# Prompt attention scores of a hybrid decoder: one 128-query matmul becomes four 32-query matmuls in four column groups

## The chip, the cores and the metric

The kernel runs on one core of one Trainium2 chip. The metric is the device time of one execution in microseconds (us), median of several runs. A profile is one execution, with its own time.

## What is computed

One inference step of a two-layer decoder for 512 prompt tokens and 8 samples of 4 tokens (544 tokens in all, model width 1024), in float32. In each layer the input projection `x @ w_in` feeds four mixers (a gated convolution A, a gated delta rule B, a gated linear attention C, a differential attention D with relative bias); their outputs are joined, projected by `w_o` and normalised, and a channel mixer follows (a dense SwiGLU in layer 0, a mixture of eight experts in layer 1). The change touches only the prompt part of mixer D:

```python
def _diff_attn_core(q, k, v, q_pos, k_pos, lam, rel_bias):
    s = jnp.einsum('bqhmd,bkhmd->bmhqk', q, k).astype(jnp.float32) * (HEAD_DIM_DQK ** -0.5)
    bias = jnp.transpose(rel_bias[_t5_bucket(q_pos, k_pos)], (2, 0, 1)).astype(jnp.float32)
    s = jnp.where(k_pos[None, :] <= q_pos[:, None], s + bias, -jnp.inf)
    p = jax.nn.softmax(s, axis=-1)
    w = p[:, 0] - lam * p[:, 1]
    return jnp.einsum('bhqk,bkhv->bqhv', w.astype(v.dtype), v)
```

There are four heads, each with two score maps (m = 0 and 1) of depth 32, and queries come in blocks of 128.

## The kernel before

One program does both layers in turn. `mixers` (L480) traces, in this order: `d_in` (projections d_q, d_k, d_v), `b_in` (L744: projections of B, convolutions, norms), `b_chunks` (L836: the delta rule), `d_attn` (L592, called at L1322: attention of the prompt and of the samples), `c_in` (L1116: projections of C), then `b_sample`, `mix_a`, `mix_c`. Projections go through `dense` (L383): for each tile of weights 48 matmuls into a tile `st`, with weights and activations each split into a high and a low part (`wh`, `wl`, `xh`, `xl`). All matmuls are issued by the helper `mm` (L291 and L292), so the profile shows them at L292 and tells them apart by their tiles.

`d_attn` alternates steps of `d_sample` (L608) with heads of the prompt: after step n of `d_sample` it traces heads until their number reaches (n+1)*16/20. A step of `d_sample` loads pages of the cache (tile `pg`) and makes scores with queries `qs` and outputs with probabilities `kv`; its matmuls come in fours, for four samples b, each into partitions 32b to 32b+31 of one PSUM tile. Another group of four of this kind, for the new tokens of the samples, multiplies `etn` with `vt` (L686). There, as in the change, 32 rows and 32 columns of the array are used by each matmul, all four have the same moving operand, and the output is 256 wide.

`d_head` (L708) is one query block (qb = 0 to 3) of one head: 16 calls in a layer, 32 in all. For each m it takes a PSUM tile from the pool `dx` (three buffers) and makes the scores: the stationary operand is 32 x 128 (q, tile `y`), the moving one 32 x nk (k, tile `arr`), with nk = 128, 256, 384 or 512 by the query block. So there are 64 score matmuls, 16 of each width. Behind them come the bias (VectorE, L295), the maximum (L726), the exponential (ScalarE, L728), the two weights, four or fewer transposes on TensorE (L736), a copy (L737) and the matmuls with `vt`.

A float32 matmul stands in the trace as two MATMUL records and two weight loads; a matmul of `st` (type fp32r) as one of each.

The order of instructions in each engine's queue is not that of the text. It is written when the program is built: `tile.TileContext(nc, schedule_with_timeline_sim=True)` (L2155) has a planner run the program on a clock of its own, and whenever an engine is free there, the planner gives it, of the instructions whose operands and buffers are there by that clock, the one that was traced first. On the chip each engine works its queue off in that order.

Of the kernel before, what the change touches and what calls it, by code (L numbers as in the profile page):

```python
# [267 lines left out]
def _body(ctx, tc, I, O):  # L268
# [22 lines left out]
    def mm(out, lhsT, rhs, start=True, stop=True):  # L291
        return PE.matmul(out, lhsT, rhs, start=start, stop=stop)  # L292

    def tt(e, out, a, b, op):
        return e.tensor_tensor(out, a, b, op=op)  # L295
# [184 lines left out]
    def mixers(l, y32, hook):  # L480
# [8 lines left out]
        def mx():  # L489
            return xps.tile([128, 512], F32, name="mx")  # L490

        def dx():
            return dps.tile([128, 512], F32, name="dx")
# [214 lines left out]
        def d_head(q, k, vt, qb, tl, h2):  # L708
            od = y32[:, 6:8]
            nk = 128 * (qb + 1)  # L710
            q0 = 128 * qb
            b0 = max(0, q0 - 128)
            h = 2 * tl + h2
            hp = slice(64 * h2, 64 * h2 + 64)

            def go():
                zz = dq.tile([128, 8], F32, name="zp", bufs=2)
                e, pss = [], []
                for m in range(2):
                    p0 = h2 * 64 + m * 32  # L720
                    ps = dx()
                    mm(ps[:, 0:nk], q[p0:p0 + 32, tl, q0:q0 + 128], k[p0:p0 + 32, tl, 0:nk])
                    pss.append(ps)
                for m, ps in enumerate(pss):
                    tt(V, ps[:, b0:nk], ps[:, b0:nk], bt[:, h, 256 - (nk - b0):256], OP.add)
                    V.reduce_max(zz[:, m:m + 1], ps[:, 0:nk], axis=AX.X, negate=True)  # L726
                    em = dq.tile([128, 512], F32, name="kv", bufs=KVB)
                    S.activation(em[:, 0:nk], ps[:, 0:nk], AF.Exp, bias=zz[:, m:m + 1], accum_out=zz[:, 2 + m:3 + m])  # L728
                    e.append(em)
                V.reciprocal(zz[:, 4:6], zz[:, 2:4])  # L730
                tt(V, zz[:, 5:6], zz[:, 5:6], neglam[:, l:l + 1], OP.mult)
                S.activation(e[1][:, 0:nk], e[1][:, 0:nk], AF.Copy, scale=zz[:, 5:6])
                V.scalar_tensor_tensor(e[0][:, 0:nk], e[0][:, 0:nk], zz[:, 4:5], e[1][:, 0:nk], op0=OP.mult, op1=OP.add)
                po, pw = pss
                for kb in range(qb + 1):
                    PE.transpose(pw[:, kb * 128:(kb + 1) * 128], e[0][:, kb * 128:(kb + 1) * 128], ident)  # L736
                S.activation(e[1][:, 0:nk], pw[:, 0:nk], AF.Copy)  # L737
                for kb in range(qb + 1):
                    mm(po[hp, 0:128], vt[:, kb, h * 64:h * 64 + 64], e[1][:, kb * 128:(kb + 1) * 128], start=kb == 0, stop=kb == qb)
                V.tensor_copy(od[hp, tl, q0:q0 + 128], po[hp, 0:128])  # L740

            return go
# [566 lines left out]
        if l:  # L1309
# [4 lines left out]
            ps = mx()  # L1314
# [853 lines left out]
```

## Time and profile before

| | us |
|---|---|
| median of 3 runs | 2140.98 |
| lowest and highest | 2140.56 to 2145.11 |
| profiled execution | 2135.03 |
| its span, first to last instruction | 2133.4 |
| mean granted TensorE clock in it | 0.958 |

The page of the profile has engine busy times, the span in 40 slices, DMA queues and the costliest groups. The stretches in which the heads of the prompt are worked on are 40 to 360 us (layer 0) and 985 to 1310 us (layer 1). In a timeline the start of a MATMUL group and the start of the group behind it tell what the group took of the engine's time: the records' own durations run on past that, since matmuls are pipelined.

### The profile page before, as it was taken

Reading aid. Unit: us, or ns where it says so; the run is one execution under the profiler, and the core shown is the slowest. Engines: PE = TensorE matmul, PEld = TensorE weight load, DVE = VectorE, ACT = ScalarE, POOL = GpSimd, SP = SyncE. Lnnn points to the kernel's source line nnn. Section 1 sums busy time; section 2 is a strip of 40 time slices with the busy share of each in tenths; the row PEclk is TensorE's granted clock in tenths of the full one; section 3 lists DMA queues with packets and bytes.
Section 4 is the critical chain, followed back from the end, with each engine's and each line's share of the span. In section 5 each row is a group of like instructions: output and inputs, shape, how many; then the busy total and the mean of one; then the engine's idle time right before and its main releaser. Section 6 shows DMA issues by size and latency. Waiting matters only on the chain. (4 is left out here: it accounts for less than half of the span.)

```text
span 2133.4 us, 46787 instructions
## 1 busy us (share of the span) xinstructions
PE 2001.4 (94%) x17620; PEld 1800.9 (84%) x17620; DVE 1298.2 (61%) x2588; ACT 946.4 (44%) x1826; POOL 375.2 (18%) x544
## 2 busy tenths in 40 slices
PE   8999989998999999989999999995999999999895
PEld 7877647987999999978687658985999999999894
DVE  4566555567333333653566566566887878767875
ACT  3444234544322223432544234534666666665441
POOL 1220032202000000031120032101220303403532
PEclk9999998989999999999999989996999999999998
DMA  6456551323222322545554543134778878787851
GB/s 238 147 155 178 148 165 42 94 88 92 90 87 75 102 85 81 150 135 170 162 150 135 170 122 99 43 109 160 230 257 307 298 224 300 228 284 258 289 182 64
DMA packets 183924, 340.93 MB, mean 160 GB/s; under 512 B 28035, under 2 KB 103912, under 8 KB 183688
## 3 DMA queue, kind: packets, MB, share of 16 engines
q1 hardware_dynamic: 160744, 287.67, 42.7%
q0 software_dynamic: 13968, 48.04, 7.2%
q10 hardware_dynamic: 8976, 2.13, 0.5%
q8 instruction: 141, 2.31, 0.4%
q14 instruction: 95, 0.78, 0.1%
HBM read 319.91 MB, written 17.85 MB: 158 GB/s over the span
## 5 line engine op out<-in xcount | busy, mean ns | idle before, releaser
L295 DVE TENSOR_TENSOR wl<-wraw,wh 128x1024 fp32r<-128x1024 f32 (+2 forms) x474 | 550.8, 1165 | 338.7 <-ACT wh L371 328.9
L371 ACT ACTIVATE wh<-wraw 128x1024 fp32r<-128x1024 f32 (+2 forms) x474 | 463.3, 980 | 493.9 <-PE st L292 267.5
L292 PE MATMUL st<-xh,wh 128*128 128x256 f32 (+1 forms) x1536 | 460.2, 300 | 20.6 <-ACT wh L371 7.6
L292 PE MATMUL st<-xl,wh 128*128 128x256 f32 (+1 forms) x1536 | 457.2, 298 | 4.0 <-DVE xl L295 4.0
L292 PE MATMUL st<-xh,wl 128*128 128x256 f32 (+1 forms) x1536 | 455.6, 297 | 4.0 <-DVE wl L295 3.8
L292 PEld LDWEIGHTS st<-xh,wh 128*128 128x128 f32 x1536 | 298.5, 195 | 37.5 <-ACT wh L371 7.7
L292 PEld LDWEIGHTS st<-xh,wl 128*128 128x128 f32 x1536 | 298.7, 195 | 14.7 <-issue 8.4
L292 PEld LDWEIGHTS st<-xl,wh 128*128 128x128 f32 x1536 | 299.1, 195 | 13.3 <-issue 7.8
L292 PE MATMUL st<-xg,wh 128*128 128x416 f32 (+4 forms) x880 | 237.9, 351 | 1.3 <-DVE m_u L1746 0.7
L292 PE MATMUL st<-xg,wl 128*128 128x208 f32 (+4 forms) x880 | 211.8, 241 | 0.0
L292 PEld LDWEIGHTS st<-xg,wl 128*128 128x128 f32 x880 | 168.0, 191 | 0.0
L292 PEld LDWEIGHTS st<-xg,wh 128*128 128x128 f32 x880 | 165.3, 188 | 2.7 <-issue 0.8
L292 PE MATMUL st<-hg,wh 128*128 128x416 f32 (+4 forms) x440 | 122.3, 355 | 0.1
L292 PE MATMUL st<-hg,wl 128*128 128x208 f32 (+4 forms) x440 | 107.9, 247 | 1.7 <-DVE wl L295 1.7
L1481 POOL TENSOR_SCALAR r<-r,par 128x256 f32<-128x256 f32 (+1 forms) x32 | 30.5, 966 | 446.4 <-ACT xh L1480 446.4
L292 PE MATMUL ff<-hh,wl 128*128 128x256 f32 (+1 forms) x352 | 102.4, 294 | 4.6 <-DVE wl L295 4.6
L292 PE MATMUL st<-wh,xg 128*128 128x256 f32 x528 | 105.5, 293 | 0.0
L292 PE MATMUL ff<-hh,wh 128*128 128x256 f32 (+1 forms) x352 | 102.5, 292 | 1.6 <-ACT wh L371 1.6
L292 PE MATMUL ff<-xh,wh 128*128 128x256 f32 (+1 forms) x352 | 102.5, 291 | 0.5 <-ACT wh L371 0.5
L292 PE MATMUL ff<-xl,wh 128*128 128x256 f32 (+1 forms) x352 | 102.4, 291 | 0.0
L292 PE MATMUL ff<-xh,wl 128*128 128x256 f32 (+1 forms) x352 | 102.2, 291 | 0.0
L292 PE MATMUL ff<-hl,wh 128*128 128x256 f32 (+1 forms) x352 | 101.8, 290 | 0.0
(581 smaller groups left out, 3956.1 us busy)
## 6 DMA issues: line engine op xcount, KB each, us to landing
pg<-in_kc_dram SPq DMA_DIRECT2D x256, 128.0 KB
pg<-in_vc_dram SPq DMA_DIRECT2D x256, 128.0 KB
wraw<-in_w_in_dram POOLq DMA_DIRECT2D x56, 512.0 KB, 4.3
wraw<-in_m_g_dram SPq DMA_DIRECT2D x54, 512.0 KB
wraw<-in_m_u_dram SPq DMA_DIRECT2D x54, 512.0 KB
wraw<-in_m_g_dram SPq DMA_DIRECT2D x65, 256.0 KB
wraw<-in_m_u_dram SPq DMA_DIRECT2D x65, 256.0 KB
wraw<-in_w_o_dram SPq DMA_DIRECT2D x32, 512.0 KB
```

The source lines that it names most:

```text
L292: return PE.matmul(out, lhsT, rhs, start=start, stop=stop)
L295: return e.tensor_tensor(out, a, b, op=op)
L371: S.activation(h, r, AF.Copy)
L1481: G.tensor_scalar(ri[:, u], ri[:, u], gcol[:, u:u + 1], bcol[:, u:u + 1], op0=OP.mult, op1=OP.add)
```

## The change

The one matmul of 128 queries becomes four of 32 queries. Each writes 32 partitions of the same PSUM tile and streams the same keys.

```diff
                 for m in range(2):
                     p0 = h2 * 64 + m * 32
                     ps = dx()
-                    mm(ps[:, 0:nk], q[p0:p0 + 32, tl, q0:q0 + 128], k[p0:p0 + 32, tl, 0:nk])
+                    for c in range(0, 128, 32):
+                        mm(ps[c:c + 32, 0:nk], q[p0:p0 + 32, tl, q0 + c:q0 + c + 32], k[p0:p0 + 32, tl, 0:nk])
                     pss.append(ps)
```

## Rows read from the trace of the kernel before

**Rows 1.** The page, part 1: busy us, share of span, instructions.

```profile
PE 2001.4 (94%) x17620; PEld 1800.9 (84%) x17620; DVE 1298.2 (61%) x2588; ACT 946.4 (44%) x1826; POOL 375.2 (18%) x544
```

**Rows 2.** Windows of both attention stretches: stretch, length, busy of each engine, clock, DMA.

```profile
40.00:360.00 320.00, 300.08 (x2949) 225.84 (x2948) 182.84 (x486) 126.07 (x293) 52.85 (x120) 0.95 0.52 150
985.00:1310.00 325.00, 308.76 (x3041) 235.28 (x3040) 190.07 (x512) 131.32 (x313) 57.27 (x130) 0.95 0.48 140
```

**Rows 3.** Waits of PE, 40 to 360 us: the longest in total; total, times, longest.

```profile
PE dx L292 <- DMA pg<-in_kc_dram: 7.4, 5, 2.9
```

**Rows 4.** Groups of instructions by form: the score matmuls.

```profile
L292 PE MATMUL dx<-arr,y 32*128 32x512 f32 x32 | 17.2, 673 | 0.0
...
L292 PE MATMUL dx<-arr,y 32*128 32x384 f32 x32 | 14.5, 533 | 0.0
...
L292 PE MATMUL dx<-arr,y 32*128 32x256 f32 x32 | 11.1, 426 | 0.0
...
L292 PE MATMUL dx<-arr,y 32*128 32x128 f32 x32 | 7.6, 332 | 0.0
```

**Rows 5.** Timelines of PE: start us, us; one score matmul of each width, its follower.

```profile
107.13 0.48 PE L292 MATMUL dx<-arr,y 32*128 32x128 f32 x2
107.54 0.40 PE L292 MATMUL st<-xh,wh 128*128 128x288 f32 x1
...
146.52 0.69 PE L292 MATMUL dx<-arr,y 32*128 32x256 f32 x2
147.14 0.39 PE L292 MATMUL st<-xh,wl 128*128 128x256 f32 x1
...
251.80 0.91 PE L292 MATMUL dx<-arr,y 32*128 32x384 f32 x2
252.64 0.73 PE L292 MATMUL mx<-lt,inv 64*64 64x64 f32 x9
...
288.75 1.12 PE L292 MATMUL dx<-arr,y 32*128 32x512 f32 x2
289.80 0.83 PE L292 MATMUL dx<-pg,qs 128*32 128x256 f32 x9
```

**Rows 6.** Timeline of PE: a group of four in one piece.

```profile
350.99 0.63 PE L292 MATMUL dx<-vt,etn 32*32 32x256 f32 x8
351.56 0.25 PE L292 MATMUL mx<-kq 64*32 64x32 f32 x4
```

**Rows 7.** Timelines of PE: the same group of four, other samples; then layer 1.

```profile
206.74 0.61 PE L292 MATMUL dx<-vt,etn 32*32 32x256 f32 x2
207.28 0.65 PE L292 MATMUL dx<-kv,vt 128*64 128x128 f32 x4
207.86 0.63 PE L292 MATMUL dx<-vt,etn 32*32 32x256 f32 x6
...
1147.18 0.61 PE L292 MATMUL dx<-vt,etn 32*32 32x256 f32 x2
```

**Rows 8.** Timelines of PE: first and last score matmuls followed by earlier text.

```profile
42.91 0.49 PE L292 MATMUL dx<-arr,y 32*128 32x128 f32 x4
43.33 0.40 PE L292 MATMUL st<-xh,wh 128*128 128x288 f32 x1
...
1244.34 1.13 PE L292 MATMUL dx<-arr,y 32*128 32x512 f32 x4
1245.40 0.92 PE L292 MATMUL dx<-pg,qs 128*32 128x256 f32 x10
```

**Rows 9.** Tile dx: weight loads, duration min/median/max in ns.

```profile
L292 PEld LDWEIGHTS dx<-arr,y x128: 181/184/332, 42.9 to 1288.6; 32*128 32x128 f32 x128
...
L292 PEld LDWEIGHTS dx<-vt,etn x32: 101/103/105, 206.7 to 1284.4; 32*32 32x32 f32 x32
```

**Rows 10.** Tile dx: who waited for it (us, times).

```profile
  DVE dx L295: 26.4, 32
```

## Prediction

> **What bounds the kernel now.** I read the page's busy times first. TensorE is busy for 94% of the span, VectorE for 61%, ScalarE for 44% [rows 1], so the first question is what the change does to TensorE's queue. An average hides stages, so I then asked for windows of the two stretches that hold all heads of the prompt. There TensorE is busy for 300.1 of 320 us and 308.8 of 325 us, while VectorE has 182.8 and 190.1, and the DMA engines are about half busy [rows 2]. The list of TensorE's waits names no large one: the longest entry of layer 0 is 7.4 us, for pages of the cache [rows 3]. So in both stretches TensorE is the bound, with 36 us of idle time in 645 us (5.6%), and what is added to its queue arrives in the end time nearly whole.
>
> The score matmuls themselves are small: by the table of groups by form they add up to 17.2 + 14.5 + 11.1 + 7.6 = 50.4 us of busy time in both layers [rows 4], and that counts the pipelined tails. What one takes of the queue is read from the timeline, from its start to the start of what follows: 0.41 us at 128 keys, 0.62 at 256, 0.84 at 384, 1.05 at 512 [rows 5]. Each further 128 keys cost 0.21 us, so streaming takes 0.21, 0.43, 0.64 and 0.85 us, and 0.2 us are fixed.
>
> **What the change does, part by part.** It removes 64 matmuls and adds 256, so TensorE has 384 more MATMUL records and as many more weight loads. Nothing else is edited: VectorE's bias addition still waits for the whole tile, now for the last of four matmuls.
>
> *If the four stay together.* The nearest row is the group of four with `etn`: the same 32 rows and 32 columns for each matmul, one moving operand for all four, 256 wide. Its eight records take from 350.99 to 351.56, 0.57 us [rows 6]. Eight records in a line would take at least 4 x 0.43 = 1.7 us of streaming, so the four column groups do run at the same time. Against 0.62 us for one matmul of 128 queries of that width [rows 5] that saves 0.05 us. The weight loads show where it comes from: 184 ns for 128 columns, 103 ns for 32 [rows 9], a difference of 81 ns of which the staggered start of the four takes some back. It does not depend on the width, so 64 x 0.05 to 0.06 = 3.2 to 3.8 us; I take -3.5.
>
> The Trainium skill ("TensorEngine Tiling (Array Packing)", Performance Considerations, When to Use Tiling) names column tiling for a stationary operand of at most 64 columns; here it has 128, which fill the array already. By that rule the four gain nothing over the one, and the sum below would be 3.5 us higher. The row shows a small gain, from the load and not from packing.
>
> *If the planner parts the four.* Four instructions can be parted, one cannot. The planner gives a free TensorE the instruction that was traced first among those that are ready, and two of the four `etn` groups show what follows: one matmul at 206.74, then two matmuls `dx<-kv,vt` of an earlier-traced head, then the other three at 207.86; in layer 1 the same happens at 1147.18 [rows 7]. On the chip the second of four starts some ns behind the first, so the planner's clock must give the first a slot of its own that is long enough for the other work to become ready in it. I take it that this clock runs the four in a line. A piece that stands alone is dear: the single `etn` matmul holds the queue from 206.74 to 207.28, 0.54 us, hardly less than all four together, since it streams all the keys. With 0.21 us for each 128 keys, one more piece costs 0.33, 0.54, 0.75 or 0.97 us at 128, 256, 384 or 512 keys.
>
> How often? In the timeline I looked up what follows each of the 64 score matmuls. An instruction from earlier text means that it was ready, by the planner's clock, when the score matmul ended; after the change that is the end of the first quarter, and the planner will put it ahead of the other three. That is so for 29 of 64: 14 of 16 at 128 keys, 2 at 256, 5 at 384, 8 at 512. Mostly these are projections and norms of B, steps of `b_chunks`, and `d_sample` steps that were traced before the head; the first is the pair at 42.91, followed by `st`, the last the pair at 1244.34, followed by `dx<-pg,qs` [rows 8]. The other 35 are followed by later text (projections of C, mostly, as at 147.14 in [rows 5]) and can stay whole. One cut each: 14 x 0.33 + 2 x 0.54 + 5 x 0.75 + 8 x 0.97 = 17.2 us. If what is left is cut again with the same share (29/64 = 0.45), the factor is 1 + 0.45 + 0.21 = 1.66, and it is 28.5 us. With the saving of 3.5: +13.7 to +25.0. I take the middle, +19, and 1 us less for the share of idle time that may swallow it: +18.
>
> The outer bounds: no cut at all, -3.5; all 64 cut into four pieces, 3 x 16 x (0.33 + 0.54 + 0.75 + 0.97) = +124.
>
> *What is queued behind.* The bias addition on VectorE waits for the last piece; it waited 26.4 us for `dx` in 32 waits [rows 10], on an engine with 40% to spare, so that costs nothing by itself. It does hold one of the three `dx` buffers longer, and the next head or step of `d_sample` waits for that buffer on TensorE. The cover is other TensorE work; I cost it at nothing and leave the loss to the second rival.
>
> **The rivals.**
>
> *The four stay together* (ends on the other side). The price is -3.5 us: 2137.5. It decides by the length of the planner's slot for one quarter: if that is a few ns, nothing becomes ready in it. For it: two of the four `etn` groups are whole [rows 6]. Against it: the two cut ones. By the rule of the skill above it would be 2141.
>
> *The planner's clock misleads it* (slower than the forecast). If the planner runs the four in a line, it counts 3 x 16 x (0.21 + 0.43 + 0.64 + 0.85) = 102 us more on TensorE than the chip needs. The softmax behind a head then seems covered by TensorE work which on the chip is soon over, and TensorE waits at the transposes of L736 or at pages. TensorE's idle time of 36 us in both stretches [rows 2] would grow; with a quarter of the 102 us, +25 on top of the forecast: 2184. For it: that clock, if rows 7 are read rightly. Against it: there is other work between the steps of a head (in rows 5 projections follow at once).
>
> *The four run in a line on the chip.* +102 us: 2243. Rows 6 speak clearly against it, but there the moving operand lies in partitions 0 to 31 only.
>
> *Another order by chance.* A changed order moves all work behind it; TensorE's waits for pages and for weights could shrink by some us. That gives about 2132.
>
> **How the numbers follow.** The profiled execution took 2135.0 us, 6 us (0.3%) below the median of 2141.0 us; the sum is made on its span, and I add it to the median, as the rows' durations do not depend on that difference. Forecast, cut in part: 2141 + 18 = 2159, chance 0.52 (from +5 to +40, with a tenth of it within 0.2%). Together: 0.20, half of it within 0.2% and half beyond it, as -3.5 us is 0.16%. Misled planner: 0.18. In a line: 0.04. By chance lower: 0.06. A change of under 0.2% (4.3 us) can hardly be told from none here. Faster by more than that: 0.10 + 0.04 = 0.14; the same: 0.10 + 0.05 + 0.01 = 0.16; slower: 0.70. The range leaves out the serial case, the upper part of the misled planner and the lowest few: 2134 to 2200.
>
> **What would show it.** In the timeline of the changed kernel, score matmuls stand as `32*32 32x512 x8` in one piece, or as x2, x4 and x6 with other tiles between. On the timeline, a piece of eight at 512 keys should take about 1.0 us and a piece of two nearly as much. Counting pieces gives the added TensorE time directly: pieces beyond 64, times the prices above. The window rows should show more TensorE busy time in both stretches, of about the size of the loss; if the loss comes with more idle time instead, the second rival is right. The prediction is wrong if nearly all stand in one piece, or if eight records at 512 keys take about 3.5 us.

## The result, and the profile after

The changed kernel takes 2151.86 us (median of 20 executions, 2139.91 to 2169.41), the kernel before, run beside it, 2139.91 us (20 executions, 2128.76 to 2160.54). The ratio is 1.0075 with a 95% interval of 1.0057 to 1.0094: 16 us slower, 12 to 20 (the two medians by themselves lie 12 us apart). All ratios here leave out executions more than 1.5% above the fastest of their kernel, which is one, the 2174.73 us below. The forecast was 18 us slower. The time came out as forecast, but, as the runs below show, not for the reason that was given; the sum landed near the time by coincidence.

The page of the changed kernel's profile: part 1 (busy us, share of the span, instructions), and the line of part 2 with the granted clock in 40 slices; its span is 2155.5 us, against 2133.4 before. The last line is the clock in the kernel before:

```profile
PE 2023.4 (94%) x18004; PEld 1807.2 (84%) x18004; DVE 1300.1 (60%) x2588; ACT 946.2 (44%) x1826; POOL 375.9 (17%) x544
...
PEclk9999988999999999999998787997999999999997
...
PEclk9999998989999999999999989996999999999998
```

Against [rows 1] TensorE is 22.0 us longer busy, as much as the span grew (22.1 us); VectorE, ScalarE and GpSimd have the busy time they had, to 2 us. The prediction had named just this as its sign. But a busy TensorE may have more to do, or do the same at a lower clock, and the 8, 7, 8, 7 in the slices from 1132 to 1347 us, in layer 1's attention, where the kernel before has 9, 9, 8, 9 in the same slices, point to the clock. The windows of the two stretches (length, busy of each engine, PEclk, DMA share, GB/s), which answer to [rows 2]:

```profile
40.00:360.00 320.00, 301.18 (x3047) 219.31 (x3047) 180.72 (x477) 122.21 (x279) 50.52 (x118) 0.93 0.51 150
985.00:1310.00 325.00, 309.49 (x3067) 230.71 (x3066) 180.92 (x484) 121.61 (x282) 51.68 (x116) 0.89 0.46 139
```

In layer 1 the clock is 0.89 where it was 0.95, and VectorE gets 484 instructions done where it got 512 done: the stage is behind. (In fixed windows TensorE's busy time hardly moves; a slower stage just runs on past the window's end.)

The score matmuls by form (busy us, mean ns), which answer to [rows 4]:

```profile
L292 PE MATMUL dx<-arr,y 32*32 32x384 f32 x128 | 18.7, 580 | 0.0
L292 PE MATMUL dx<-arr,y 32*32 32x512 f32 x128 | 14.7, 657 | 0.0
L292 PE MATMUL dx<-arr,y 32*32 32x256 f32 x128 | 11.4, 386 | 0.0
L292 PE MATMUL dx<-arr,y 32*32 32x128 f32 x128 | 6.3, 280 | 0.0
```

And pieces of TensorE's timeline (start, us, tile, count), which answer to [rows 5] and [rows 8]; they come in order of time, with gaps:

```profile
42.51 0.43 PE L292 MATMUL dx<-arr,y 32*32 32x128 f32 x10
42.86 0.40 PE L292 MATMUL st<-xh,wh 128*128 128x288 f32 x1
...
73.99 0.41 PE L292 MATMUL dx<-arr,y 32*32 32x128 f32 x6
74.33 0.40 PE L292 MATMUL st<-xh,wh 128*128 128x288 f32 x1
...
86.80 0.42 PE L292 MATMUL dx<-arr,y 32*32 32x128 f32 x8
87.15 1.19 PE L292 MATMUL mx<-row,cst 128*128 128x256 f32 x4
...
171.10 0.63 PE L292 MATMUL dx<-arr,y 32*32 32x256 f32 x8
171.67 0.40 PE L292 MATMUL st<-xh,wl 128*128 128x288 f32 x1
...
228.26 0.84 PE L292 MATMUL dx<-arr,y 32*32 32x384 f32 x6
229.03 1.05 PE L292 MATMUL dx<-pg,qs 128*32 128x256 f32 x10
230.01 0.83 PE L292 MATMUL dx<-arr,y 32*32 32x384 f32 x2
230.77 0.39 PE L292 MATMUL st<-xh,wh 128*128 128x256 f32 x1
...
294.32 1.06 PE L292 MATMUL dx<-arr,y 32*32 32x512 f32 x8
295.31 0.44 PE L292 MATMUL mx<-gst,arr 64*128 64x64 f32 x4
```

Three readings. A whole group (x8) holds the queue for 0.35, 0.57 and 0.99 us at 128, 256 and 512 keys; the one matmul took 0.41, 0.62 and 1.05 [rows 5]. So 0.05 to 0.06 us are saved, as predicted. A group that is cut, as at 228.26, takes 0.77 + 0.76 us in two pieces where a whole one of 384 keys takes 0.78: the price of a lone piece, 0.75, is as predicted too. But cuts are few. In TensorE's queue, as the planner wrote it, 55 of the 64 groups stand whole, among them that at 86.80, though `mx<-row,cst`, text traced earlier, follows it. Cut are nine, each once: three at 128 keys, three at 256, three at 384, none at 512. (The x10 at 42.51 is a whole group and the first quarter of the next, whose other three follow at 73.99.) They cost at most 3 x (0.33 + 0.54 + 0.75) = 4.9 us. Three more look broken in the timeline, where records of small matmuls of other tiles start between those of one group; in the queue these are whole. Groups give back 64 x 0.06 = 3.8 us. So neither the cuts nor the new shape make 16 us.

Where they are lost, the clock shows. Windows of 1167 to 1208 us, first of the kernel before, then of the changed one (same columns as above):

```profile
1167.00:1208.00 41.00, 40.81 (x577) 30.50 (x576) 23.80 (x46) 12.72 (x27) 1.38 (x4) 0.96 0.51 154
...
1167.00:1208.00 41.00, 40.12 (x382) 26.74 (x383) 15.98 (x32) 8.18 (x18) 0.00 (x0) 0.50 0.29 85
```

TensorE is busy all through in both, yet in the changed kernel the granted clock is 0.50, the lower of its two levels (1.2 GHz), for the whole 41 us, and it has 382 MATMUL records in place of 577. The program alone does not fix this. The changed kernel was profiled once more (`changed_again` below), and there the same window reads:

```profile
1167.00:1208.00 41.00, 40.21 (x510) 28.61 (x512) 24.65 (x52) 14.30 (x31) 2.12 (x3) 0.97 0.49 143
```

So one stretch of one execution shows that the clock can cost this much, and not what costs it. What does differ between the two programs in every execution, beside the shape, is the order: the planner has written another one. Compared instruction by instruction, with a group of four counted as one, TensorE's queue differs from its 536th matmul on, in 3574 of 14586 places; VectorE's differs in 845 of 2588, ScalarE's in 379 of 1749.

### The profile page after: what moved, and what is told of

It reads as the page before. It is cut to its first block, busy times and chain, and to the rows that moved or that the text cites. A ratio compares the mean times of both kernels' runs of the same rounds, so it can differ in the third digit from the quotient of the medians.

```text
span 2155.5 us, 47593 instructions
## 1 busy us (share of the span) xinstructions
PE 2023.4 (94%) x18004; PEld 1807.2 (84%) x18004; DVE 1300.1 (60%) x2588; ACT 946.2 (44%) x1826; POOL 375.9 (17%) x544
## 5 line engine op out<-in xcount | busy, mean ns | idle before, releaser
L295 POOL TENSOR_TENSOR m_g<-m_g,m_u 128x208 f32<-128x208 f32 (+4 forms) x55 | 50.9, 926 | 303.4 <-DVE m_u L1747 270.4
```

## The experiments

Three causes could be told apart: (A) the order that the planner wrote for all other work, (B) the new shape of the matmuls itself, (C) the cuts. For that I wrote the queue order of every engine out, by edges that say only "after this one", so that shape and order can be combined at will. A group of four counts there as one unit, so none is cut. Each kernel is timed beside the kernel before on the same chip.

**The new shape in the order of before.** The edit is the change itself, and the order of the kernel before (`ORDER_OF` holds it for each engine):

```diff
+    edge = mybir.DependencyInfo(mybir.DependencyClass.NoSync, mybir.DependencyReason.DATA)
+    for e, s in ORDER_OF.items():
...
+        for a, b in zip(seq, seq[1:]):
+            tc.add_manual_dep(b, a.name, edge, reason="order")
```

> The scores are made by four matmuls of 32 queries as in the changed kernel, but every engine's queue keeps the order of the kernel before; each group of four stands in one piece where the one matmul stood. Theory A (the loss of 0.75% comes from the new order that the planner wrote, by way of a granted clock that stays at half speed longer): the order is the old one, so 2136 to 2141 us, ratio 0.998 to 1.000, half-speed time near the 183 us of before. Theory B (32 x 32 matmuls by themselves lower the granted clock or run slower in this place): about 2152, ratio 1.005 to 1.009, half-speed time well over 183 us in both attention stretches. Theory C (the loss is what cut groups cost): 2136 to 2141, as no group is cut.

Measured: 2137.2 us (2128.55 to 2144.63, 12 executions) against 2142.5 (35): ratio 0.9969, interval 0.9945 to 0.9992. The new shape alone makes the kernel faster, by 5 us (1.7 to 11.8 by the interval), which takes in the 3.5 us of the sum. B falls.

**The old shape in the order of the changed kernel.** Edges as above, now from the changed kernel's queues, around the one matmul of 128 queries. Beside the edges it differs from the changed kernel in this:

```diff
-                    for c in range(0, 128, 32):
-                        mm(ps[c:c + 32, 0:nk], q[p0:p0 + 32, tl, q0 + c:q0 + c + 32], k[p0:p0 + 32, tl, 0:nk])
+                    mm(ps[:, 0:nk], q[p0:p0 + 32, tl, q0:q0 + 128], k[p0:p0 + 32, tl, 0:nk])
```

> The scores are made by one matmul of 128 queries as before, but every engine's queue has the order of the changed kernel; where a group of four was cut there, the one matmul stands at the place of the first piece. Theory A (order): 2150 to 2158 us, ratio 1.005 to 1.009. Theory B (shape): about 2140, ratio 0.998 to 1.002. Theory C (cuts): about 2140, as there is nothing to cut.

Measured: 2158.77 us (2146.0 to 2167.08, 12); ratio 1.0065, interval 1.0039 to 1.0091. Not one of the four-matmul groups is in this kernel, and the whole loss is there. The median is 1 us above the range that was expected, the ratio within it. A stands.

**The new shape in the new order, nothing cut**, and **the changed kernel once more** beside it:

> The changed kernel's order on every engine, four matmuls of 32 queries, but each group in one piece (at the place of its first piece). About a dozen groups are cut in the changed kernel. Theory A (order) and theory B (shape): 2147 to 2154 us, ratio 1.004 to 1.008, a few us under the changed kernel at most. Theory C (cuts): about 2138, ratio 0.998 to 1.000.

> The changed kernel itself beside the other three on one chip: 2152 us, ratio 1.006 to 1.009 by its measurement; all theories agree. Its half-speed time in the profile is asked for: 243 us were seen in one execution against 183 us before; theory A and theory B expect well over 200 us again, theory C about 183.

Measured: 2155.98 us (2141.32 to 2174.73, 12), ratio 1.0060 (1.0032 to 1.0089), without cuts; 2155.0 us (2145.95 to 2171.98, 12), ratio 1.0066 (1.0038 to 1.0095), with them. The first lies 2 us above its range, by the median. Cuts are worth nothing that can be measured: C falls. One expectation was missed: the profiled execution of the changed kernel is here the fastest of its twelve, and spent about 200 us of the whole program at half speed (clock 0.953 over 2144.2 us), nearer to the kernel before in its profile (about 180) than to the changed kernel in its first (about 240), where A and B expected well over 200. Over all twelve executions the mean is 219 us, over the 35 of the kernel before 196.

**Which layer.** The two orders coincide in the middle of layer 0's channel mixer, so each half can be taken from either kernel. First the changed kernel's order up to there and the old one behind, then the reverse; both with four matmuls in whole groups. The edit is that of the new shape in the order of before, with other numbers in `ORDER_OF`.

> Four matmuls of 32 queries, no group cut; every queue has the changed kernel's order up to the middle of layer 0's feed-forward part, where both orders coincide, and from there the order of the kernel before. Theory A1 (the new order costs its time in layer 1's attention stretch alone): as with the whole old order, 2134 to 2141 us, ratio 0.995 to 0.999. Theory A2 (it costs time in both layers alike): 2144 to 2150 us, ratio 1.001 to 1.004.

> The same with the halves exchanged: the order of the kernel before up to the middle of layer 0's feed-forward part, the changed kernel's order behind it. Theory A1: 2152 to 2158 us, ratio 1.004 to 1.008, with half-speed time of TensorE's clock of 60 to 110 us in layer 1's attention against 34 and 48 in the old order. Theory A2: 2144 to 2150 us, ratio 1.001 to 1.004.

Measured: 2137.84 us (12), ratio 0.9983 (0.9968 to 0.9999), with the new order in layer 0; 2155.7 us (8), ratio 1.0061 (1.0037 to 1.0086), with it in layer 1. The loss is that of layer 1 alone.

**What the layer-1 stage consists of.** The stretch from layer 1's first `dx` matmul to its first matmul of the channel mixer, one window in each kernel: start and end, length, TensorE busy, ..., PEclk. In order: before; four in the old order; new order in layer 0; changed; changed again; one in the new order; new order in layer 1; four whole in the new order.

```profile
972.12:1400.61 428.49, 409.51 (x4338) 323.79 (x4338) 244.37 (x640) 182.31 (x447) 76.49 (x170) 0.95 0.43 126
...
972.52:1402.23 429.71, 412.23 (x4530) 323.91 (x4529) 245.22 (x641) 182.09 (x447) 76.75 (x170) 0.93 0.43 126
...
970.09:1399.62 429.53, 410.94 (x4529) 323.40 (x4529) 245.29 (x641) 182.05 (x447) 76.69 (x170) 0.94 0.43 127
...
972.96:1420.84 447.88, 429.81 (x4530) 336.14 (x4530) 246.61 (x640) 182.69 (x447) 77.87 (x170) 0.89 0.40 121
...
968.27:1406.28 438.01, 416.30 (x4530) 325.82 (x4530) 246.38 (x640) 182.38 (x447) 77.63 (x170) 0.93 0.42 124
...
976.29:1424.87 448.58, 425.22 (x4338) 336.74 (x4338) 246.07 (x640) 183.17 (x447) 76.93 (x170) 0.91 0.41 120
...
973.62:1419.96 446.34, 423.52 (x4530) 332.69 (x4530) 247.10 (x641) 183.33 (x447) 77.13 (x170) 0.90 0.42 122
...
966.61:1430.93 464.32, 443.46 (x4530) 343.78 (x4529) 246.49 (x641) 183.00 (x447) 77.43 (x170) 0.86 0.40 117
```

Length less busy time is TensorE's idle time; the time at the lower level is 2 x (1 - PEclk) x length, since that level is half of the other. Between the first and the last row the length grows by 35.8 us, idle time by 1.9, half-speed time from 42.8 to 130.0: so 33.9 / 87.2 = 0.39 us are lost in each us at half speed. With that factor every row comes apart in the same way:

```
kernel                     length   idle   half-speed   length - idle - 0.39 x half-speed
before                      428.5   19.0        43            393
four, old order             429.7   17.5        60            389
new order in layer 0        429.5   18.6        52            391
changed                     447.9   18.1        99            391
changed, again              438.0   21.7        61            392
one, new order              448.6   23.4        81            394
new order in layer 1        446.3   22.8        89            389
four whole, new order       464.3   20.9       130            393
```

What is left is 389 to 394 us in all eight (PEclk has two digits, which alone is worth 2 us), whatever the shape, the cuts and the order. So in these profiles the order costs through TensorE's clock, with some idle time beside it. All executions together say nearly the same: by their spans and clocks, four in whole groups spent 229 us of the whole program at half speed in the new order and 192 in the old, and 37 x 0.39 = 14 of the 18 us between their mean times; the other 4 us are not the clock's. That is an accounting; the next pair moves the clock on purpose.

**More matmuls that do nothing.** Into both orders go 288 full-array matmuls whose results nothing reads, in layer 1 only, six ahead of each score and of the first transpose of each head (`fours` lists what stands in one piece; `fill` is made ahead of the transposes, the last line stands behind them):

```diff
-                    mm(ps[:, 0:nk], q[p0:p0 + 32, tl, q0:q0 + 128], k[p0:p0 + 32, tl, 0:nk])
+                    fours.append([mm(ps[:, 0:256], xh[0][:, f, 0:128], xh[0][:, f, 0:256]).ins.name for f in range(6 * l)] + [mm(ps[c:c + 32, 0:nk], q[p0:p0 + 32, tl, q0 + c:q0 + c + 32], k[p0:p0 + 32, tl, 0:nk]).ins.name for c in range(0, 128, 32)])
...
+                fill = [mm(pw[:, 0:256], xh[0][:, f, 0:128], xh[0][:, f, 0:256]).ins.name for f in range(6 * l)]
...
+                fours.append(fill[:6 * l + 1])
```

> Four matmuls of 32 queries in the order of the kernel before (as four_old_order), and 288 more matmuls in layer 1's attention whose results are thrown away: six (full array, 256 columns, as the st projections) ahead of each of the 32 scores and of the first transpose of each of the 16 heads. An st matmul of that size follows the one before it after 0.12 us in the timeline, so they hold TensorE for about 288 x 0.12 = 35 us. Theory (the loss of an order is TensorE's time at half clock): the fillers take half-speed time away in that stretch (58 us from the first score to the experts in the profile of four_old_order), and the time is 2137 + 35 less up to 0.38 x 58 = 22: 2150 to 2172. Rival (the order costs by something else, and the clock only goes with it): 2172 as well, so this run is the yardstick for filled_new_order.

> The same 288 thrown-away matmuls at the same scores and transposes, in the order of the changed kernel (as four_new_order_whole). Without them this order is 19 us above the other (2156 against 2137). Theory (half clock is what the order costs): where the fillers lift the clock, the distance to filled_old_order shrinks to 0 to 10 us, and the stretch from the first score to the experts follows 391 + 35 + idle time + 0.38 x half-speed time in both. Rival (something else): the distance stays at 15 to 25 us though the half-speed time falls. If the half-speed time does not fall below what these two orders had without fillers (58 and 133 us in their profiles), the pair tells nothing.

Measured: 2172.99 us in the old order (2159.05 to 2180.89, 4; ratio 1.0171, 1.0136 to 1.0205), 2174.07 in the new one (2168.43 to 2177.78, 4; ratio 1.0160, 1.0127 to 1.0193). The two orders, 19 us apart without the added matmuls, are 1 us apart with them. The first lies 1 us above its range, at the end where the clock gives nothing back. The window of the stage in both, first old, then new order:

```profile
963.97:1420.64 456.67, 443.51 (x4818) 354.91 (x4818) 247.72 (x641) 182.33 (x447) 76.66 (x170) 0.96 0.40 119
...
963.21:1433.13 469.92, 452.09 (x4818) 364.09 (x4817) 246.51 (x641) 183.43 (x448) 78.34 (x170) 0.94 0.40 116
```

In the new order half-speed time fell from 130 to 56 us though TensorE has more to do, in the old one from 60 to 37. Idle time and 0.39 x half-speed taken off, 429 and 430 us are left, 41 and 37 us more than in the same orders above, the price of the added matmuls (35 was expected). Over all executions the median clock rose from 0.9465 to 0.955 in the new order, from 0.9555 to 0.9575 in the old one. In the old order they cost 36 us of the median, nearly all of that; in the new one only 18, and the risen clock accounts for most of the rest. This is the causal test: with the order kept and the clock raised, the loss of the order is gone, as far as four executions each can tell: the medians are sure to about 7 us, the distance of the two to about 10. The two profiles above are 13 us apart, since that of the old order is the fastest of its four executions (2159.05).

**Other splits, planned afresh.** Two matmuls of 64 queries, and four of 32 only at 512 keys, both in the order that the planner then writes. The edits are shown against the changed kernel:

```diff
-                    for c in range(0, 128, 32):
-                        mm(ps[c:c + 32, 0:nk], q[p0:p0 + 32, tl, q0 + c:q0 + c + 32], k[p0:p0 + 32, tl, 0:nk])
+                    for c in range(0, 128, 64):
+                        mm(ps[c:c + 64, 0:nk], q[p0:p0 + 32, tl, q0 + c:q0 + c + 64], k[p0:p0 + 32, tl, 0:nk])
```

> Two matmuls of 64 queries in place of four of 32, and the planner writes the order anew; it is a third order, about as far from both others as they are from each other. If the size of the matmuls were what costs the time, this would lie between the two kernels, 2142 to 2150 us. If the order decides, which the planner changes with any small change of its clock, then the result has no tie to the size: anything from 2130 to 2160 us, with the granted clock telling which (about 0.956 at 2137, 0.947 at 2157).

```diff
-                    for c in range(0, 128, 32):
-                        mm(ps[c:c + 32, 0:nk], q[p0:p0 + 32, tl, q0 + c:q0 + c + 32], k[p0:p0 + 32, tl, 0:nk])
+                    for c in range(0, 128, 32 if qb == 3 else 128):
+                        w_ = 32 if qb == 3 else 128; mm(ps[c:c + w_, 0:nk], q[p0:p0 + 32, tl, q0 + c:q0 + c + w_], k[p0:p0 + 32, tl, 0:nk])
```

> Four matmuls of 32 queries only for the last query block (512 keys, 16 of the 64 score matmuls), one of 128 for the others; the planner writes the order, which stays much nearer to that of the kernel before (about a third as many places differ). Theory A (order): between 2132 and 2145 us, ratio 0.996 to 1.002, by the share of the order that stays. A theory in which each group of four costs something by itself would give a quarter of the 16 us, most at 512 keys: 2146 us or more.

Measured: 2163.46 us (2151.42 to 2173.49, 6; ratio 1.0103, 1.0072 to 1.0135) and 2155.84 us (2149.67 to 2168.28, 6; ratio 1.0061, 1.0039 to 1.0083). The first lies 3 us above what I expected (2130 to 2160). The second missed it (2132 to 2145) by 11: I had thought that so small a change would leave the order nearly alone. It changes 1096 of TensorE's places, about a third of what the full change does, and costs as much. By itself this time would also suit the rival named there, a price of each group of four (2146 or more); four in the old order, which cost nothing, speak against that, and the loss does not grow with the edit, as such a price would make it. Their windows of the stage, two of 64 first:

```profile
979.11:1426.71 447.60, 420.10 (x4402) 329.07 (x4402) 245.67 (x640) 183.91 (x447) 77.58 (x170) 0.92 0.42 121
...
977.59:1428.67 451.08, 426.86 (x4386) 337.12 (x4386) 245.54 (x640) 183.22 (x447) 75.81 (x170) 0.91 0.42 120
```

Idle 27.5 and 24.2 us, half-speed 72 and 81: here idle time has a larger part in it than in the changed kernel. What is left is 392 and 395 us.

The fastest kernel of the study is the change in the order of before, 2137.2 us: below the kernel before by 0.3%, below the changed kernel timed beside it (2155.0) by 0.8%. The new order in layer 0 alone, 2137.84 us, can't be told from it.

## Why the prediction was right in time and wrong in its reason

*TensorE is the bound* [rows 1, 2]: right. In all kernels of the tables the stage is the same TensorE work, its idle time and its clock, to within 3 us, and the added matmuls where there are some.

*Four kept together save 0.05 to 0.06 us, 3.5 us in all*: right, by the pieces of the timeline. Two pairs of runs in one order each agree: 2142.5 to 2137.2 in the old, and 2158.8 to 2156.0 in the new, which is within its noise. The rule of the Trainium skill that was weighed there ("TensorEngine Tiling (Array Packing)", When to Use Tiling: column tiling for up to 64 columns) would have had no gain. The row it was weighed against gave the better number: the load of 32 columns takes 104 ns in the changed kernel too (184 for 128 columns in [rows 9]).

*A lone piece costs 0.33 to 0.97 us*: right (0.75 at 228.26 and 230.01).

*29 of 64 groups are cut, some again, +17.2 to +28.5 us*: this is the step that failed. Nine were cut and none again, none at 512 keys, where eight had been counted for 7.8 us of the 17.2; at 128 keys three in place of 14. At most 4.9 us of cuts stand against 3.8 us saved, so the sum without the order is near nothing. The failing sentences are "I take it that this clock runs the four in a line" and the one by which the end of the score matmul becomes "the end of the first quarter". I had read them from two cut `etn` groups [rows 7] and left the two whole ones [rows 6] to a rival. The kind of cut was read rightly: in all nine, everything between the pieces was traced earlier. But 15 whole groups have earlier text right behind them (86.80 is one), so the quarter's slot on the planner's clock was mostly not long enough for that text to come in. How long it is stays open.

*Misled planner, with more idle time at transposes and pages*: not seen in the changed kernel, whose stage has 18.1 us idle against 19.0.

*Another order by chance*: this is what happened, and I had given it a chance of 0.06 and only the good side, "about 2132". The term was mis-sized because I priced a new order by the waits alone. The prediction's own windows had the other price in them: a clock of 0.95 in both stretches [rows 2] is 0.05 x 2 x 645 = 65 us at half speed that a new order can lengthen or shorten. Its sign was open; its size, in the kernels of the first table that have the new order in layer 1, is 18 to 87 us of half-speed time more than before, so 7 to 34 us. A rival of that size on both sides should have held much of the chance. That it came out near +18 is luck.

*"Loss as more TensorE busy time"* was met and proved nothing: busy time has the clock in it. The sign that could tell the two apart was the other one in the same paragraph, that most groups would stand in one piece, and that one said "wrong".

Still open: why the planner's order turned at the 536th matmul (I have only that a group of four, of two, or of four at one width each turn it another way), and which part of the layer-1 order lowers the clock. The added full-array matmuls raised it, but no run moved a part of the order by itself.

## What to carry to other kernels

Where a planner orders the whole program, an edit of one line has two prices, its own and that of a new order; take them apart by holding the order fixed under the new code, and the new order around the old code. Forecast the second as a spread on both sides, from what a stage loses now to waits and to the clock, and not from the edit. And read busy time beside the granted clock: a busy engine that takes longer need not be one with more to do.

## What the runs showed of the hardware

A busy TensorE can stay at its lower clock: 41 us at 0.50, with 40.1 us busy, in the changed kernel. A us at that level lost 0.39 us in this stage (33.9 / 87.2 above). The Trainium skill ("TensorE: Matmul & The Clock Gate", Terms) puts the penalty at the throttled time times one less the clock's share, which is 0.5 here. The runs show less, and do not show why.

The clock is not fixed by the program. Twelve executions of the changed kernel range from 2145.95 us at a mean clock of 0.953 to 2171.98 us at 0.938, and its two profiled executions have 99 and 61 us of half-speed time in the same stage. So one profile can't price an order; the medians over executions can.

More work may cost less than its length: some 37 us of added matmuls lengthened the kernel in the new order by 18.

Two score matmuls whose 32 rows are different ones can run side by side, which the sum left out: with the two maps of a head in a line, two took 0.42 us at 42.91 and 1.06 us at 1244.34 [rows 8], where one takes 0.41 and 1.05 [rows 5] (not always: at 305.69 two in a line took 1.63 us). In the changed kernel the ten records at 42.51 hold the queue for 0.35 us, as eight do. So a quarter right behind the group of the other map cost next to nothing; in most heads other work stands between the two maps.
